# A hybrid attention, convolution and FFN layer on one core: rows of the normed input at one address remainder, halves of 272 + 256 and 258 columns, and another order of loads

## The chip, the cores and the metric

One Trainium2 chip, one core. The metric is the device time of one execution in microseconds. Times of before are the median, lowest and highest of 3 runs. The profiled execution is a run of its own, with a time of its own.

## The reference, cut to what matters

One decoder layer on 512 tokens of width 2048, all in float32. 16 meta tokens stand in front, so the input stage works on L = 528 columns; the output has the last 512.

```python
n = _rmsnorm(h, g_mix)                       # h: 16 meta tokens + 512 tokens, 2048 wide
q, k, v, gb, gc, u = split(n @ w_in)         # six parts of 1024
o_attn = stick_breaking(rmsnorm(q), rmsnorm(k), v)     # 8 heads of 128
o_conv = gb * causal_dwconv(gc * u, conv_w)            # 3 taps, 1024 channels
h = h + concat(rmsnorm(o_attn), rmsnorm(o_conv)) @ w_out
n2 = _rmsnorm(h, g_ffn)
h = h + (silu(n2 @ w_gate) * (n2 @ w_up)) @ w_down     # 5632 wide
return h[:, 16:]
```

## The kernel before, in words

Everything is kept transposed: channels on the 128 partitions, tokens along a row. Each float32 operand is split into a high and a low float32r part, and each product is three matmuls, high·high, high·low, low·high. ScalarE and VectorE make the parts of the weights (`split_quad`, L188 and L189: `s_buf` from `w_buf`) a few quads ahead of their use; SyncE loads `w_buf` (`load_at`, L172) as places come free. The order of everything is the order in which the program is written, with three exceptions: `after(n, work)` puts work behind n further k-tiles (`tick` counts them down), `tc.high_priority` moves work ahead, and a tile is written only when the readers of what lay in its place are through.

**x.** `split_x` (L347) writes for each of 16 k-tiles two tiles of 128 x 528, `nh` and `nl`, with one row of 2112 bytes per partition each.

**Heads.** For each of 8 heads the products k, q and v are made by `product_steps` (L280, L282, L284): k and v over all 528 columns as two matmuls of 264 (H = L // 2, one per PSUM bank), q over 512 (names pk, pq, pv). The first k and q (`pk0`, `pq0`) are made while x is still being loaded and split. `qk_norm` and `attend` are put behind some k-tiles of later products.

**Convolution.** Two of the eight conv heads (CONV_FIRST = 2) are made in the plain way: c and u (pcu) as two matmuls of 260 columns, b (pb) as one of 512. Their results are stored to DRAM (`od`). The other six go by a 2 x 2 block scheme with seven products rather than eight: `form_blocks` makes four mixed blocks of x and stores them in DRAM (`fc`), with blocks of 8 k-tiles x CH = 260 columns (two 260s from column C0 = 8). Three of them are loaded into `blk` (L701), the fourth over columns 268 to 527 of the first 8 k-tiles of `nh` and `nl` (L708), all by GpSimd's queue. `pair_product` then makes, for each pair of heads and each of c, u and b, seven block products of 8 k-tiles x 3 matmuls (L742 to L744): y from n, x from `blk`, z from `blk`, x from `blk`, and z, x, x from n. `conv_taps` and `conv_out` finish on VectorE and ScalarE.

**Output projection.** `wide_product` (L842 to L844, po) reads `oc` (conv) and `oa` (attention), 512 columns at a time. The six conv heads of the block scheme lie in SBUF: four in `oc_mid`, the last two in places 0 and 1 of `oc_end`. The first two conv heads and the eight attention heads are loaded from `od` by GpSimd (L812), the conv ones into places 2 and 3 of `oc_end`. `scale_c` (its sums over partitions are `ss_c`, L636 and L637) makes the conv group's norm and is put behind 3 k-tiles of the first product.

**FFN.** The residual's norm gives blocks f0 to f6, each 8 k-tiles x 256 columns, high and low, in rows of 1024 bytes. f3, f4 and f6 go through DRAM (`fx`): they are stored tile by tile (L991, L997), and at the last tile 7 of their 8 k-tiles are loaded back, f6 in two halves by SyncE (L977), f3 and then f4 in two halves each by GpSimd (L980). f4 lies in a pool of its own (`fpool_4`), f3 and f6 in another (`fpool_last`), both where tiles of the output projection lay. Then come 44 pairs of gate and up, seven products each (y from f5, x f0, z f1, x f2, z f3, x f4, x f6, L742 to L744), and the down projection of the same form from `first` and `ring`.

Of the kernel before, what the change touches and what calls it, by code (L numbers as in the profile page):

```python
# [33 lines left out]
def hybrid_layer(ctx: ExitStack, tc: tile.TileContext, xT, w_in, w_out, w_gu, w_down, vecs, out):  # L34
# [23 lines left out]
    sm = open_pool("sm", 4, space=PSUM)  # L58

# [262 lines left out]
    H = L // 2  # L322
    n_hl = []
# [6 lines left out]
    def x_scale():  # L330
        ve.tensor_tensor(acc, acc, accs[1], ALU.add)
        for a in (0, H):
            ps = small(f"ssx{a}")
            pe.matmul(ps[:, :H], ones, acc[:, a : a + H], start=True, stop=True)
            ve.tensor_scalar(ms[:, a : a + H], ps[:, :H], 1.0 / D, EPS, ALU.mult, ALU.add)
# [11 lines left out]
    def split_x(k):  # L347
        nh = npool.tile([P, L], F32R, tag=f"nh{k}", name=f"nh{k}")
        nl = npool.tile([P, L], F32R, tag=f"nl{k}", name=f"nl{k}")
        g = g_mix[:, k : k + 1]  # L350
        sc.activation(nh, xts[k], AF.Copy, scale=g)
        ve.scalar_tensor_tensor(nl, xts[k], g, nh.bitcast(F32), ALU.mult, ALU.subtract)
        n_hl.append((nh, nl))

    def square_x(k):
# [55 lines left out]
    C0, CH = 8, (L - 8) // 2  # L411
    fc = dram.tile([P, 4, 2, 8, CH], F32R, name="fc")

    def form_blocks(k):

        x4 = stage.tile([P, 4, CH], F32, tag="x4", name=f"x4_{k}")
        st = stage.tile([P, 8 * CH], F32R, tag="st", name=f"st4_{k}").rearrange("p (i a t) -> p i a t", i=4, a=2)
        for i, kk in ((0, k), (2, k + 8)):
            nc.sync.dma_start(x4[:, i : i + 2], two(xT[kk][:, C0:]))
# [26 lines left out]
    def qk_norm(ps, g, cols, dst, parts_of, name):  # L446
# [33 lines left out]
    def head(h):  # L480

        if h:
            pk = pp.tile([P, 2, 512], F32, tag="pp", name=f"pk{h}")
            product([(pk[:, 0, :H], 0, H), (pk[:, 1, :H], H, L)], n_hl)
        else:
            pk = pk0
        kn = kns[0]
        kh = apool.tile([P, 384], F32R, tag="kh", name=f"kh{h}")
        kl = apool.tile([P, 384], F32R, tag="kl", name=f"kl{h}")
        after(8 if h else 11, qk_norm(halves(pk, H), g_k, L, kn[:, :L], (kh, kl, 384), f"k{h}"))  # L490
# [12 lines left out]
        product([(pv[:, 0, :H], 0, H), (pv[:, 1, :H], H, L)], n_hl)  # L503
        vt = t512(L, "e", 2)
        ve.tensor_tensor(two(vt[:, :L]), halves(pv, H), two(r), ALU.mult)
        after(6 if h else 11, lambda: attend(h, kn, kh, kl, qn, qh, ql, vt))
# [146 lines left out]
    def conv_taps(j, c1, c2, y):  # L653

        ve.tensor_tensor(c1, c1, two(r2[:, C0:]), ALU.mult)
        ve.tensor_tensor(c1, c2, c1, ALU.mult)
        cu = c1.rearrange("p a b -> p (a b)")
        o = META - 2 - C0
        sc.activation(y, cu[:, o : o + SEQ], AF.Copy, scale=cw[:, 3 * j : 3 * j + 1])
        for t in (1, 2):  # L660
            ve.scalar_tensor_tensor(
                y, cu[:, o + t : o + t + SEQ], cw[:, 3 * j + t : 3 * j + t + 1], y, ALU.mult, ALU.add
            )
# [12 lines left out]
    for j in range(CONV_FIRST):  # L676
# [14 lines left out]
        if j == 0:  # L691
# [14 lines left out]
    for k in range(8):  # L706
        for part in range(2):
            gp.dma_start(n_hl[k][part][:, C0 + CH :], fc[:, 1, part, k])  # L708

    def parts_of(kk, a):  # L710
        return lambda part, k: n_hl[kk + k][part][:, a : a + CH]

    def of_blk(i):
        return lambda part, k: blk[:, i, part, k]

    conv_acts = [
        parts_of(0, C0), of_blk(2), of_blk(0), of_blk(1), parts_of(0, C0 + CH), parts_of(8, C0), parts_of(8, C0 + CH)
# [69 lines left out]
    def pair(acts):  # L787
        c1, c2 = halves_of("e"), halves_of("e2")
# [4 lines left out]
    for j in range(CONV_FIRST, HEADS, 2):  # L793
        ys = []
        for m in range(2):
            c1, c2 = pair(conv_acts)
            ys.append(t512(SEQ, "v", 2)[:, :SEQ])
            conv_taps(j + m, two(c1), two(c2), ys[m])
        gbs = pair(conv_acts)
        if j < HEADS - 2:  # L800
            slots = [oc_mid[:, j + m - CONV_FIRST] for m in range(2)]
        else:
# [3 lines left out]
            oc_end = o_slots(oc2_pool, "oc_end", 4)  # L806
# [71 lines left out]
    after(3, scale_c)  # L878
# [26 lines left out]
    for i, j in enumerate(OUT_TILES):  # L905
# [35 lines left out]
        if i == KT - 1:  # L941
# [292 lines left out]
```

## Time and profile before

| what | value |
|---|---|
| median of 3 runs | 2044.49 us (2041.42 to 2046.47) |
| profiled execution, its time | 2048.55 us |
| profiled execution, its span | 2046.8 us |
| its mean granted TensorE clock | 0.998 |
| PE busy | 2032.0 us, 99% of the span, 16158 instructions |
| DVE, ACT, POOL busy | 84%, 51%, 19% |
| DMA | 361.70 MB, mean 177 GB/s |

How to read it: the span is the profiled work, and the execution's own time has 1.75 us around it. Matmuls overlap in the array, so a record of one lasts longer than the step from one start to the next; the step is what the time is made of. A PEclk of 1.00 is 2.4 GHz and 0.50 is 1.2 GHz.

### The profile page before, as it was taken

Reading aid. Unit: us, or ns where it says so; the run is one execution under the profiler, and the core shown is the slowest. Engines: PE = TensorE matmul, PEld = TensorE weight load, DVE = VectorE, ACT = ScalarE, POOL = GpSimd, SP = SyncE. Lnnn points to the kernel's source line nnn. Section 1 sums busy time; section 2 is a strip of 40 time slices with the busy share of each in tenths; the row PEclk is TensorE's granted clock in tenths of the full one; section 3 lists DMA queues with packets and bytes.
Section 4 is the critical chain, followed back from the end, with each engine's and each line's share of the span. In section 5 each row is a group of like instructions: output and inputs, shape, how many; then the busy total and the mean of one; then the engine's idle time right before and its main releaser. Section 6 shows DMA issues by size and latency. Waiting matters only on the chain.

```text
span 2046.8 us, 39727 instructions
## 1 busy us (share of the span) xinstructions
PE 2032.0 (99%) x16158; PEld 1969.1 (96%) x16158; DVE 1718.8 (84%) x2202; ACT 1051.1 (51%) x1517; POOL 381.2 (19%) x533
## 2 busy tenths in 40 slices
PE   9999999999999999999999999999999999999999
PEld 8999999999998888999999999999999999999999
DVE  8788878588876777998998998998998998888887
ACT  7666666344443435545555545554554544444443
POOL 0111111210015441011111111111101252223111
PEclk9999999999999999999999999999999999999999
DMA  6333344743365556566565565555555999989864
GB/s 230 100 129 116 127 138 130 254 149 104 104 211 181 184 181 205 155 174 171 150 176 150 151 175 153 154 171 158 151 174 152 274 311 314 246 237 255 231 156 89
DMA packets 161591, 361.70 MB, mean 177 GB/s; under 512 B 13568, under 2 KB 73216, under 8 KB 161408
## 3 DMA queue, kind: packets, MB, share of 16 engines
q1 hardware_dynamic: 79200, 227.94, 34.8%
q0 software_dynamic: 82208, 131.23, 24.4%
q8 instruction: 127, 2.08, 0.4%
q14 instruction: 56, 0.46, 0.1%
HBM read 278.50 MB, written 80.61 MB: 175 GB/s over the span
## 4 chain that ended last, share of the span: by engine, by line
PE 92%; DVE 3%; ACT 2%; DMA 2%; issue 2%; POOL 1%; SPq 0%; DVEq 0%; ACTq 0%; POOLq 0%
PE x L742 13%; PE x L744 13%; PE x L743 13%; PE z L742 6%; PE z L743 6%; PE z L744 6%; PE y L743 3%; PE y L742 3%; PE y L744 3%; PE po L843 2%; PE po L842 2%; PE po L844 2%; PE pv L280 2%; PE pv L284 1%; PE pv L282 1%
## 5 line engine op out<-in xcount | busy, mean ns | idle before, releaser
L188 ACT CAST s_buf<-w_buf 128x1024 fp32r<-128x1024 f32 (+2 forms) x665 | 660.5, 993 | 772.6 <-PE x L743 348.7
L189 DVE TENSOR_TENSOR s_buf<-w_buf,s_buf 128x1024 fp32r<-128x1024 f32 (+2 forms) x665 | 767.8, 1155 | 173.9 <-ACT s_buf L188 173.4
L743 PE MATMUL x<-f,s_buf 128*128 128x256 f32 x1408 | 388.5, 276 | 4.2 <-DMA f<-fx 4.2
L742 PE MATMUL x<-f,s_buf 128*128 128x256 f32 x1408 | 388.5, 276 | 0.5 <-ACT sides L772 0.5
L744 PE MATMUL x<-f,s_buf 128*128 128x256 f32 x1408 | 388.4, 276 | 0.0
L201 DVE TENSOR_TENSOR w_buf<-w_buf 128x1024 f32<-128x1024 f32 (+1 forms) x243 | 277.6, 1142 | 14.2 <-DMA w_buf<-w_in 9.9
L743 PEld LDWEIGHTS x<-f,s_buf 128*128 128x128 f32 x1408 | 265.4, 188 | 4.4 <-DMA f<-fx 4.4
L742 PEld LDWEIGHTS x<-f,s_buf 128*128 128x128 f32 x1408 | 265.3, 188 | 1.2 <-ACT sides L772 0.9
L744 PEld LDWEIGHTS x<-f,s_buf 128*128 128x128 f32 x1408 | 265.4, 188 | 0.0
L1036 POOL DMA_DIRECT2D fd<-s x147 | 104.0, 926 | 713.0 <-DVE s L295 691.8
L742 PE MATMUL z<-f,s_buf 128*128 128x256 f32 x704 | 193.6, 275 | 0.0
L743 PE MATMUL z<-f,s_buf 128*128 128x256 f32 x704 | 193.6, 275 | 0.0
L744 PE MATMUL z<-f,s_buf 128*128 128x256 f32 x704 | 193.6, 275 | 0.0
L744 PE MATMUL x<-ring,s_buf 128*128 128x256 f32 x608 | 167.3, 275 | 0.9 <-DVE s_buf L189 0.9
L742 PE MATMUL x<-ring,s_buf 128*128 128x256 f32 x608 | 167.2, 275 | 0.0
L743 PE MATMUL x<-ring,s_buf 128*128 128x256 f32 x608 | 167.2, 275 | 0.0
L744 PEld LDWEIGHTS z<-f,s_buf 128*128 128x128 f32 x704 | 132.1, 188 | 0.0
L743 PEld LDWEIGHTS z<-f,s_buf 128*128 128x128 f32 x704 | 132.1, 188 | 0.0
L742 PEld LDWEIGHTS z<-f,s_buf 128*128 128x128 f32 x704 | 132.1, 188 | 0.0
L1106 POOL DMA_DIRECT2D out_T<-d x62 | 60.3, 1002 | 300.4 <-DVE d L1114 240.7
L744 PEld LDWEIGHTS x<-ring,s_buf 128*128 128x128 f32 x608 | 114.1, 188 | 1.1 <-DVE s_buf L189 1.1
L743 PEld LDWEIGHTS x<-ring,s_buf 128*128 128x128 f32 x608 | 114.1, 188 | 0.0
(378 smaller groups left out, 5259.4 us busy)
## 6 DMA issues: line engine op xcount, KB each, us to landing
w_buf<-w_gu SPq DMA_DIRECT2D x176, 512.0 KB, 3.4
w_buf<-w_in SPq DMA_DIRECT2D x92, 512.0 KB, 3.4
fd<-s POOLq DMA_DIRECT2D x147, 256.0 KB, 5.2
w_buf<-w_down SPq DMA_DIRECT2D x96, 384.0 KB, 4.9
ring<-fd POOLq DMA_DIRECT2D x42, 768.0 KB, 9.1
w_buf<-w_out SPq DMA_DIRECT2D x32, 512.0 KB, 3.6
out_T<-d POOLq DMA_DIRECT2D x62, 256.0 KB, 5.6
fc<-st SPq DMA_DIRECT2D x8, 1040.0 KB, 6.2
```

Source lines behind the costliest of these rows:

```text
L188: sc.copy(hi, src)
L189: in_turn(ve.tensor_tensor(lo, src, hi.bitcast(F32), ALU.subtract), turn)
L201: in_turn(ve.tensor_tensor(sums[name], a, b, ALU.add), turn)
L280: pe.matmul(ps, wh, ah[:, a:b], start=k == 0, stop=False)
L742: pe.matmul(p, hi[:, kk], act(0, k), start=start and j == k == 0, stop=False, skip_group_check=skip)
L743: pe.matmul(p, hi[:, kk], act(1, k), start=False, stop=False, skip_group_check=skip)
L744: pe.matmul(p, lo[:, kk], act(0, k), start=False, stop=k == n - 1, skip_group_check=skip)
L842: pe.matmul(ps, hi[:, kk], ah, start=k == order[0], stop=False)
L843: pe.matmul(ps, hi[:, kk], al, start=False, stop=False)
L844: pe.matmul(ps, lo[:, kk], ah, start=False, stop=k == order[-1])
L1036: gp.dma_start(fd[c][s][:, :, k], t[:, :, i])
L1106: gp.dma_start(two(out[j]), c, accum_op=ALU.add)
```

## The change

- **One tile for the two rows of x.** `split_x` makes one tile per k-tile, of 2 x 576 columns; high and low rows of 530 columns stand in it from column 12, so they are 2304 bytes apart and all 32 rows have the same address modulo 256 bytes.
- **k and v in 272 + 256 columns.** H = 272 rather than 264. `row_of` puts the two pieces next to each other across the two PSUM banks, so that `qk_norm` and `attend` read one row of 528 (before: two of 264).
- **Conv blocks of 258 columns.** C0 = 14 and C1 = 270, CH = 258: two halves that overlap by 2 columns. c and u are made in 258 columns, b in the last 256 of them (`last_of`). `blk` has rows of 288 columns, high and low next to each other (1152 bytes apart; 2304 from k-tile to k-tile), and is loaded in runs of 1032 bytes, not 4160. `form_blocks` loads x in four pieces of 258, not two of 520. `conv_taps` multiplies by `r2` in two operations of 258 (before: one of 520).
- **The loads of two conv results.** `oc_end` is two tiles: `oc_end` (the last two block heads) and `oc_01` (the first two heads, loaded from `od`). `scale_c` is put behind 13 k-tiles, not 3.
- **The loads of f3 and f6.** SyncE loads k-tiles 0 to 5 of f3 ahead of f6; GpSimd loads k-tile 6 of f3 alone, then f4.
- The scratch memory for descriptors of GpSimd's DMAs is 8192 bytes, not 16384.

The diff, cut to its core:

```diff
-    H = L // 2
+    H, ROW = META + T2, 2304 // 4
...
-        nh = npool.tile([P, L], F32R, tag=f"nh{k}", name=f"nh{k}")
-        nl = npool.tile([P, L], F32R, tag=f"nl{k}", name=f"nl{k}")
+        n = npool.tile([P, 2 * ROW], F32R, tag=f"n{k}", name=f"n{k}")
+        n_row = n.rearrange("p (a t) -> p a t", a=2)[:, :, 12 : 14 + L]
+        nh, nl = (n_row[:, i, :L] for i in range(2))
...
+    def row_of(ps):
+
+        flat = ps.rearrange("p a b -> p (a b)")
+        return flat[:, 512 - H : 512 - H + L], [(flat[:, 512 - H : 512], 0, H), (flat[:, 512 : 512 + L - H], H, L)]
...
-    C0, CH = 8, (L - 8) // 2
+    C0 = META - 2
+    C1, CH = C0 + T2, L - C0 - T2
...
-            product([(pk[:, 0, :H], 0, H), (pk[:, 1, :H], H, L)], n_hl)
+            product(row_of(pk)[1], n_hl)
...
-        ve.tensor_tensor(c1, c1, two(r2[:, C0:]), ALU.mult)
+        for m, c in enumerate((C0, C1)):
+            ve.tensor_tensor(c1[:, m], c1[:, m], r2[:, c : c + CH], ALU.mult)
...
-            product([(p[:, 0, :CH], C0, C0 + CH), (p[:, 1, :CH], C0 + CH, L)], n_hl)
+            product([(p[:, 0, :CH], C0, C0 + CH), (p[:, 1, :CH], C1, L)], n_hl)
...
-            blk = blk_pool.tile([P, 3, 2, 8, CH], F32R, name="blk")
-            for i, n in ((2, 3), (0, 0), (1, 2)):
+            blk = blk_pool.tile([P, 8 + 48 * 288], F32R, name="blk")
+            blk = blk[:, 2 : 2 + 48 * 288].rearrange("p (i k a t) -> p i k a t", i=3, k=8, a=2)
+            pad(blk_pool, 128)
+            for i, n in enumerate((3, 0, 2)):
                 for part in range(2):
-                    gp.dma_start(blk[:, i, part], fc[:, n, part], max_dma_last_dim=4160)
+                    gp.dma_start(blk[:, i, :, part, :CH], fc[:, n, part])
...
-            gp.dma_start(n_hl[k][part][:, C0 + CH :], fc[:, 1, part, k])
+            gp.dma_start(n_rows[k][:, part, C0 + CH :], fc[:, 1, part, k])
...
-        gbs = pair(conv_acts)
+        gbs = pair([last_of(act) for act in conv_acts], T2)
...
-            oc_end = o_slots(oc2_pool, "oc_end", 4)
+            oc_end = o_slots(oc2_pool, "oc_end", 2)
+            oc_01 = o_slots(oc2_pool, "oc_01", CONV_FIRST)
...
-    after(3, scale_c)
+    after(13, scale_c)
...
-            for part in range(2):
-                nc.sync.dma_start(acts[6][:, part, :7].bitcast(F32), fx[6][:, part, :7].bitcast(F32), max_dma_last_dim=4096)
-            for s in (3, 4):
-                for part in range(2):
-                    gp.dma_start(acts[s][:, part, :7], fx[s][:, part, :7], max_dma_last_dim=4096)
+            for s, n in ((3, 6), (6, 7)):
+                for part in range(2):
+                    nc.sync.dma_start(acts[s][:, part, :n].bitcast(F32), fx[s][:, part, :n].bitcast(F32), max_dma_last_dim=4096)
+            gp.dma_start(acts[3][:, :, 6], fx[3][:, :, 6])
+            for part in range(2):
+                gp.dma_start(acts[4][:, part, :7], fx[4][:, part, :7], max_dma_last_dim=4096)
...
-    nc = bacc.Bacc("TRN2", target_bir_lowering=False, num_devices=1)
+    nc = bacc.Bacc("TRN2", target_bir_lowering=False, num_devices=1, dynamic_dma_scratch_size=8192)
```

GpSimd's queue at the end of the output projection, before; `w227` and `w229` are the residual's last two tiles, `st6` the last mixed blocks, `fd` a later stage:

```order
L1000 DMA out_T<-w223_7761 128x512
L314 TENSOR_TENSOR acc_h_6624<-acc_h_6624,w226_7785 128x512
L900 DMA w229_7822<-xT 128x512
L997 DMA fx3_6636<-st6_7780 256x1x256
L997 DMA fx4_6637<-st6_7780 256x1x256
L980 DMA f3_7935<-fx3_6636 128x2x896 x2
L980 DMA f4_7925<-fx4_6637 128x2x896 x2
L1036 DMA fd0_0_7962<-s0_2_8211 256x1x256
```

The same place after the change:

```order
L1017 DMA out_T<-w223_7767 128x512
L317 TENSOR_TENSOR acc_h_6630<-acc_h_6630,w226_7791 128x512
L916 DMA w229_7828<-xT 128x512
L1014 DMA fx3_6642<-st6_7786 256x1x256
L1014 DMA fx4_6643<-st6_7786 256x1x256
L995 DMA f3_7941<-fx3_6642 128x2x256
L997 DMA f4_7931<-fx4_6643 128x2x896 x2
L1053 DMA fd0_0_7969<-s0_2_8218 256x1x256
```

Two large loads of f3 have left this queue; one small one stands in their place, and the two loads of f4 follow it.

SyncE's queue at that place, before (the rows are its loads of weights, of f6 and two stores of the output):

```order
L172 DMA w_buf_111<-w_gu 128x1024 x4
L977 DMA f6_7936<-fx6_6638 128x2x896 x2
L1000 DMA out_T<-w227_7817 128x512
L172 DMA w_buf_111<-w_gu 128x1024
L1000 DMA out_T<-w229_7822 128x512
```

And after the change:

```order
L175 DMA w_buf_111<-w_gu 128x1024 x4
L994 DMA f3_7941<-fx3_6642 128x2x768 x2
L994 DMA f6_7942<-fx6_6644 128x2x896
L1017 DMA out_T<-w227_7823 128x512
L175 DMA w_buf_111<-w_gu 128x1024
L994 DMA f6_7942<-fx6_6644 128x2x896
L1017 DMA out_T<-w229_7828 128x512
```

The two loads of f3 stand ahead of f6 here, and the second half of f6 has moved behind an output store and a load of weights.

TensorE at the end of the first product of the output projection, before; `ss_c` is the conv group's sum of squares:

```order
L842 MATMUL po0_6639<-oc_end_6582,s_buf_112 128x512
L843 MATMUL po0_6639<-oc_end_6582,s_buf_112 128x512
L844 MATMUL po0_6639<-oc_end_6582,s_buf_112 128x512
L842 MATMUL po0_6639<-oc_end_6582,s_buf_112 128x512
L636 MATMUL ss_c_6660<-w167_6654,ones_r_107 128x512
L843 MATMUL po0_6639<-oc_end_6582,s_buf_112 128x512
```

After the change:

```order
L863 MATMUL po0_6645<-oc_01_6588,s_buf_112 128x512
L861 MATMUL po1_6646<-oc_end_6587,s_buf_112 128x512
L862 MATMUL po1_6646<-oc_end_6587,s_buf_112 128x512
L863 MATMUL po1_6646<-oc_end_6587,s_buf_112 128x512
L649 MATMUL ss_c_6696<-w167_6690,ones_r_107 128x512
L650 MATMUL ss_c_6696<-w168_6691,ones_r_107 128x512
L861 MATMUL po1_6646<-oc_end_6587,s_buf_112 128x512
```

`ss_c` has moved back by five matmuls: it stood within the last k-tile of po0, and now stands behind the first k-tile of po1.

## Rows read from the trace of the kernel before

**Rows 1.** The page's busy time by engine, whole span.
```profile
PE 2032.0 (99%) x16158; PEld 1969.1 (96%) x16158; DVE 1718.8 (84%) x2202; ACT 1051.1 (51%) x1517; POOL 381.2 (19%) x533
```

**Rows 2.** Waits of PE: who waited for what, us in total, times, longest us.
```profile
PE x L743 <- DMA f<-fx: 4.2, 1, 4.2
...
PE ss_c L636 <- ACT w L294: 1.1, 1, 1.1
PE x L744 <- DVE s_buf L189: 1.1, 2, 0.9
```

**Rows 3.** PE by windows (length, busy, records): pk, pq, pcu, pairs, po, FFN.
```profile
221.12:228.12 7.00, 7.00 (x60) 1.00 0.87 273
231.55:234.32 2.77, 2.77 (x14) 1.00 0.56 189
381.29:388.50 7.21, 7.21 (x62) 1.00 0.90 305
449.09:466.37 17.28, 17.28 (x147) 1.00 0.33 116
699.67:763.00 63.33, 63.33 (x281) 1.00 0.58 177
1000.02:1600.02 600.00, 600.00 (x5297) 1.00 0.55 159
```

**Rows 4.** PE's timeline where the pq window starts: start, duration, instruction.
```profile
231.29 0.29 PE L584 MATMUL c<-bh,ones_r 128*128 128x288 f32 x1
231.42 0.29 PE L585 MATMUL c<-bl,ones_r 128*128 128x288 f32 x1
231.55 0.40 PE L280 MATMUL pq<-nh,s_buf 128*128 128x512 f32 x1
```

**Rows 5.** The chain of waits around the loads of f3 and f4.
```profile
774.98 0.45 POOL f L980
...
777.13 16.11 DMA f<-fx
793.28 0.58 PE x L743
```

**Rows 6.** Windows behind that wait: length, PE, PEld, DVE, ACT, POOL, PEclk, DMA, GB/s.
```profile
793.28:798.35 5.07, 5.07 (x23) 5.07 (x24) 0.00 (x0) 0.00 (x0) 0.00 (x0) 0.50 0.29 103
798.35:799.13 0.78, 0.78 (x3) 0.64 (x3) 0.42 (x1) 0.71 (x1) 0.00 (x0) 0.57 0.00 0
```

**Rows 7.** DMA, 763 to 794 us: rate; then queue, count, KB, us to landing.
```profile
DMA packets 3229, 9.38 MB, mean 303 GB/s; under 512 B 240, under 2 KB 752, under 8 KB 3227
...
f<-fx POOLq DMA_DIRECT2D x4, 896.0 KB, 11.1
...
f<-fx SPq DMA_DIRECT2D x2, 896.0 KB, 8.3
```

**Rows 8.** The chain of waits, 600 to 610 us, around ss_c.
```profile
605.48 1.31 POOL acc_c L314
...
606.81 0.63 ACT w L294
...
607.48 0.50 PE ss_c L636
607.98 0.23 PE po L843
```

**Rows 9.** Windows, columns as in rows 6: loads of blk, of n, conv pairs.
```profile
382.00:405.00 23.00, 23.00 (x191) 22.91 (x190) 12.31 (x15) 7.70 (x12) 4.70 (x7) 1.00 1.02 368
405.00:416.00 11.00, 11.00 (x50) 8.98 (x50) 5.61 (x6) 3.09 (x5) 8.49 (x16) 1.00 1.01 236
416.00:600.00 184.00, 183.23 (x1520) 182.37 (x1519) 152.23 (x167) 88.02 (x118) 15.41 (x15) 1.00 0.37 122
```

**Rows 10.** DMA, 407 to 416 us, as in rows 7: loads of n.
```profile
DMA packets 2242, 2.26 MB, mean 251 GB/s; under 512 B 251, under 2 KB 2186, under 8 KB 2241
...
nh<-fc POOLq DMA_DIRECT2D x7, 130.0 KB, 3.2
```

More of the change, by code (lines that the diff above doesn't have):

```diff
@@ L332, in x_scale @@
         for a in (0, H):
-            ps = small(f"ssx{a}")
-            pe.matmul(ps[:, :H], ones, acc[:, a : a + H], start=True, stop=True)
-            ve.tensor_scalar(ms[:, a : a + H], ps[:, :H], 1.0 / D, EPS, ALU.mult, ALU.add)
+            b = L if a else H
+            ps = small(f"ssx{a}")[:, : b - a]
+            pe.matmul(ps, ones, acc[:, a:b], start=True, stop=True)
+            ve.tensor_scalar(ms[:, a:b], ps, 1.0 / D, EPS, ALU.mult, ALU.add)
         rsqrt(r, ms, L)
@@ L418, in form_blocks @@
         for i, kk in ((0, k), (2, k + 8)):
-            nc.sync.dma_start(x4[:, i : i + 2], two(xT[kk][:, C0:]))
+            for m, c in enumerate((C0, C1)):
+                nc.sync.dma_start(x4[:, i + m], xT[kk][:, c : c + CH])
         for i, kk in ((0, k), (2, k + 8)):
@@ L455, in qk_norm @@
         cuts = [(0, cols)] if cols == SEQ else [(0, H), (H, L)]
-        raw_v, s_v = (raw, s) if cols == SEQ else (two(raw), two(s))
-        sc.activation(s_v, ps, AF.Square)
-        sc.activation(raw_v, ps, AF.Copy, scale=g)
+        sc.activation(s, ps, AF.Square)
+        sc.activation(raw, ps, AF.Copy, scale=g)
         split(sh, sl, s)
@@ L489, in head @@
         kl = apool.tile([P, 384], F32R, tag="kl", name=f"kl{h}")
-        after(8 if h else 11, qk_norm(halves(pk, H), g_k, L, kn[:, :L], (kh, kl, 384), f"k{h}"))
+        after(8 if h else 11, qk_norm(row_of(pk)[0], g_k, L, kn[:, :L], (kh, kl, 384), f"k{h}"))
         if h:
@@ L502, in head @@
         pv = pp.tile([P, 2, 512], F32, tag="pp", name=f"pv{h}")
-        product([(pv[:, 0, :H], 0, H), (pv[:, 1, :H], H, L)], n_hl)
+        pv_row, parts = row_of(pv)
+        product(parts, n_hl)
         vt = t512(L, "e", 2)
-        ve.tensor_tensor(two(vt[:, :L]), halves(pv, H), two(r), ALU.mult)
+        ve.tensor_tensor(vt[:, :L], pv_row, r, ALU.mult)
         after(6 if h else 11, lambda: attend(h, kn, kh, kl, qn, qh, ql, vt))
@@ L653, in conv_taps @@
     def conv_taps(j, c1, c2, y):
-        ve.tensor_tensor(c1, c1, two(r2[:, C0:]), ALU.mult)
+        for m, c in enumerate((C0, C1)):
+            ve.tensor_tensor(c1[:, m], c1[:, m], r2[:, c : c + CH], ALU.mult)
         ve.tensor_tensor(c1, c2, c1, ALU.mult)
-        cu = c1.rearrange("p a b -> p (a b)")
-        o = META - 2 - C0
-        sc.activation(y, cu[:, o : o + SEQ], AF.Copy, scale=cw[:, 3 * j : 3 * j + 1])
+        y = two(y)
+        sc.activation(y, c1[:, :, :T2], AF.Copy, scale=cw[:, 3 * j : 3 * j + 1])
         for t in (1, 2):
             ve.scalar_tensor_tensor(
-                y, cu[:, o + t : o + t + SEQ], cw[:, 3 * j + t : 3 * j + t + 1], y, ALU.mult, ALU.add
+                y, c1[:, :, t : t + T2], cw[:, 3 * j + t : 3 * j + t + 1], y, ALU.mult, ALU.add
             )
@@ L707, in hybrid_layer, with last_of @@
         for part in range(2):
-            gp.dma_start(n_hl[k][part][:, C0 + CH :], fc[:, 1, part, k])
+            gp.dma_start(n_rows[k][:, part, C0 + CH :], fc[:, 1, part, k])
     def parts_of(kk, a):
-        return lambda part, k: n_hl[kk + k][part][:, a : a + CH]
+        return lambda part, k: n_rows[kk + k][:, part, a : a + CH]
     def of_blk(i):
-        return lambda part, k: blk[:, i, part, k]
+        return lambda part, k: blk[:, i, k, part, :CH]
+    def last_of(act):
+        return lambda part, k: act(part, k)[:, CH - T2 :]
     conv_acts = [
-        parts_of(0, C0), of_blk(2), of_blk(0), of_blk(1), parts_of(0, C0 + CH), parts_of(8, C0), parts_of(8, C0 + CH)
+        parts_of(0, C0), of_blk(0), of_blk(1), of_blk(2), parts_of(0, C0 + CH), parts_of(8, C0), parts_of(8, C1)
     ]
@@ L785, in pair_product, with pair @@
         return x
-    def pair(acts):
-        c1, c2 = halves_of("e"), halves_of("e2")
+    def pair(acts, n):
+        c1, c2 = (halves_of(t)[:, : 2 * n] for t in ("e", "e2"))
         x = pair_product(acts, two(c1), two(c2), sides)
@@ L810, in hybrid_layer @@
             with tc.high_priority():
-                for name, t in [(f"c{m}", oc_end[:, 2 + m]) for m in range(2)] + [(f"a{h}", oa_all[:, h]) for h in range(HEADS)]:
+                for name, t in [(f"c{m}", oc_01[:, m]) for m in range(2)] + [(f"a{h}", oa_all[:, h]) for h in range(HEADS)]:
                     gp.dma_start(t, od[name])
         for m in range(2):
-            s = t512(SEQ, "e", 2)[:, :SEQ] if j == HEADS - 2 else cpool.tile([P, SEQ], F32, tag="s", name=f"sq{j}_{m}")
+            s = t512(SEQ, "e", 2)[:, :SEQ] if j == HEADS - 2 else gbs[m]
             with tc.high_priority(1 << 20) if j == HEADS - 2 else ExitStack():
-                conv_out(j + m, gbs[m][:, META - C0 :], ys[m], slots[m][:, 0], slots[m][:, 1], s, ve)
-    oc = [oc_end[:, 2], oc_end[:, 3], *(oc_mid[:, i] for i in range(HEADS - 2 - CONV_FIRST)), oc_end[:, 0], oc_end[:, 1]]
+                conv_out(j + m, gbs[m], ys[m], slots[m][:, 0], slots[m][:, 1], s, ve)
+    oc = [oc_01[:, 0], oc_01[:, 1], *(oc_mid[:, i] for i in range(HEADS - 2 - CONV_FIRST)), oc_end[:, 0], oc_end[:, 1]]
     oc_order = (*range(CONV_FIRST, HEADS), *range(CONV_FIRST))
```

11 lines of the change are left out of this document (6 added, 5 removed).

## The prediction

> **What bounds the kernel now.** I read four views in this order. First the busy times: PE is busy for 2032.0 of 2046.8 us [rows 1], so the time is what TensorE's steps take, and only 14.8 us are left to win from its pauses. Then PE's waits: one stands out, 4.2 us for the load of an FFN block; the next two, 1.1 us for `ss_c` and 1.1 us for a weight split, are small [rows 2]. Then the length of a step, which the mean duration of a record can't show, since records overlap; I read it from windows cut at the start of a matmul and ending at the start of another [rows 3]. A window also counts the records still running at its start: at 231.55 the two of 231.29 and 231.42, 0.29 long each, are still open [rows 4], so its 14 records are 12 steps. With two off each: pk 7.00 us / 58 = 120.7 ns for 264 columns, pq 2.77 / 12 = 230.8 for 512, pcu 7.21 / 60 = 120.2 for 260, the conv pairs 17.28 / 145 = 119.2 for 260, po 63.33 / 279 = 227.0 for 512, the FFN 600.00 / 5295 = 113.3 for 256.
>
> The reader is to see that these are two rates at one granted clock of 1.00. The FFN takes 113.3 / 256 = 0.443 ns a column, po 0.443, and at that rate 264 columns take 116.9, 260 take 115.1, 512 take 226.7. All products that read `nh`, `nl` or `blk` are 3.8 to 5.1 ns a step above it. What sets these apart in the code is the row of the moving operand: f rows of 1024 bytes and oa, oc rows of 2048 are whole multiples of 256 bytes, rows of 2112 (n) and 1040 (blk) are not, so there the address modulo 256 changes from matmul to matmul. That the remainder is the cause is my inference; no row of before varies it alone.
>
> Last the chain of waits and the windows around the 4.2 us, which hold more than the wait itself.
>
> **The rows of x and the widths.** Steps that the change touches, counted from the loops:
>
> - k and v: 8 heads x 2 products x 16 k-tiles x 3 x 2 pieces = 1536, less the first k (96), made while x still comes in: 1440. At 272 + 256 the mean is 264 as before. Full gain 120.7 - 116.9 = 3.8 ns, 5.5 us. But the two pieces start at columns 0 and 272, 1088 bytes apart, so two remainders 64 bytes apart still alternate. Between no gain and 5.5 I take half, 2.7 us.
> - q: 384 less 48 in the start, and b of two heads, 96: 432 steps of 512. All start at one remainder now. 230.8 - 227.0 = 3.8 ns, 1.6 us, taken whole, since po shows the rate at this width.
> - plain c, u: 384 steps, 120.2 to 258 x 0.443 = 114.2: 6.0 ns, 2.3 us, taken whole; columns 14 and 270 lie 1024 bytes apart.
> - conv pairs: 9 pair products x 7 blocks x 24 = 1512 steps. Six of nine have 258 columns (1008 steps, 119.2 - 114.2 = 5.0 ns), three have 256 (504, 5.9 ns): 8.0 us in full. Four of seven blocks read n rows: 4.6 us, taken whole. Three of seven read `blk`, where high and low rows lie 1152 bytes apart, 128 modulo 256: at most 3.4 us, of which 0.8 is columns alone; I take that and half of the rest, 2.1.
>
> Sum: 2.7 + 1.6 + 2.3 + 4.6 + 2.1 = 13.3 us; bounds 2.1 us (columns alone: (384 x 2 + 1008 x 2 + 504 x 4) x 0.443 ns) and 17.4.
>
> The Trainium skill speaks against this term: "SBUF — State Buffer", section "Who interferes with whom", gives TensorE two read ports of its own, for the moving operand and for the weights, and says that it waits on nobody; then address would not matter. By that rule the sum would be 2.1. The trace disagrees: 512 columns took 230.8 ns from n and 227.0 from oa.
>
> **The loads of f3 and f4.** GpSimd issues f3 and f4 from 774.98 on; the transfer ends at 793.28, and PE has waited 4.2 us, so f4 was wanted at 789.1 [rows 2, 5]. Behind the wait TensorE is granted 0.50 for 5.07 us and 0.57 for 0.78 [rows 6]: of the 26 steps there, 24 of 256 columns and 2 of 512 take 24 x 0.1133 + 2 x 0.227 = 3.17 us at full clock, so 5.85 - 3.17 = 2.7 us more. A pause of 4.2 us went ahead of that fall of the clock. Together 6.9 us.
>
> Before, 4 x 896 KB = 3.67 MB went through GpSimd's queue, in 18.3 us from the first issue to 793.28; at the stretch's 303 GB/s [rows 7] 5.5 MB moved in that time, so about 1.9 MB were others'. After, GpSimd has 256 + 2 x 896 KB = 2.1 MB. With the same 1.9 MB beside it that is 13.2 us, landing at about 788.4, 0.7 us ahead of need. f3's first six k-tiles ride ahead of f6 on SyncE's queue, and its seventh is the first thing GpSimd sends. SyncE's queue then holds 2 x 768 + 896 - 2 x 896 = 640 KB more ahead of its next load of weights, 2.2 us at that rate; splits are made some quads ahead, which hides it; without that cover it costs those 2.2 us. f6's second half moves behind one load of weights; f6 is the last block to be read. I take 6.6 us of 6.9; the ends are 3 us (f4 lands 3 us late and the clock still falls in part) and 7.1.
>
> **The loads of two conv results and ss_c.** PE waits 1.1 us for the chain acc_c 1.31, square root and scale 0.63 [rows 2, 8]. After the change `ss_c` stands 5 matmuls of 0.227 later, 1.1 us. I take 0.9, ends 0.3 and 1.3. The separate `oc_01` lets its loads be issued without waiting for readers of `oc_end`'s place; nothing on PE waits for them in the rows, so nothing is counted.
>
> **Small edits.** `r2` in two operations: 8 more on VectorE, each under the mean there of 152.23 / 167 = 0.91 us, so under 7.3 us in all; VectorE idles 184 - 152.23 = 31.8 us in the six block heads [rows 9]. Nothing counted; without that cover up to 0.5 us per pair. `form_blocks` issues 16 more loads on SyncE, whose bytes do not grow, and is early. PSUM rows in one piece: nothing.
>
> **blk in runs of 1032 bytes.** Before, the six loads ran at 368 GB/s, and n's 16 loads, of runs near 1 KB, at 236 to 251 [rows 9, 10]. Now all are of that kind: 6.2 MB of blk, 2.1 of n and about 3 of others are 11.3 MB at 251 GB/s = 45 us from 382, ending at 427. The first block, y, starts where the last of these windows does, at 416, and takes 24 steps; x from `blk` follows at about 419, when 6.2 MB and a third of the others' bytes, 29 us' worth, should be in (411). n's new columns are first read after four blocks (4 x 24 x 0.119 = 11.4 us), at 427.4 or a little later. Cost 0, up to 4 if the rate is lower.
>
> **Sum.** 13.3 + 6.6 + 0.9 = 20.8 us off the profiled execution's 2048.55: 2027.8. That execution stands 4.06 us above the median of the three runs, so on the median 2023.7, say **2024**.
>
> **Rivals.**
> (1) *All moved rows reach the fast rate*, k, v and blk too, 17.4 + 6.9 + 1.3 = 25.6: 2019. For: one alternation of two remainders may do no harm; against: in rows 3 nothing with two remainders is fast. Chance 0.18.
> (2) *Only width counts.* The rate belongs to something other than the address, say to the splits going on beside it; then columns alone, 2.1 + 6.6 + 0.9 = 9.6: 2035. For: pq and po differ in more than the address. Against: po, pq and pcu run beside splits alike. Chance 0.17.
> (3) *blk or n comes late*, by up to 4 us, and the clock falls by part: 20.8 - 4 to 7 us, 2028 to 2031. Chance 0.08.
> (4) *Slower: GpSimd's descriptors.* Half the scratch memory might let one load's descriptors fit in place of two, so that its queue goes one load at a time: descriptors, transfer, landing in a row. Then each blk load costs its 1040 KB at 251 GB/s, 4.2 us, plus up to 6 of the rest, six of them 63 us, and 16 of n about 3.7 us each, 60: the n rows come at 382 + 63 + 60 = 505 rather than 430, 75 us late, and the time is about 2100. It decides from the point where the 22 loads take over 48 us. For: runs four times shorter want four times the descriptors; against: GpSimd is busy only 4.70 of the 23 us of blk's loads [rows 9]. Chance 0.04.
> (5) *The load doesn't move.* f4 still waits for the readers of its place and f3's late piece, and 4 us of the 6.9 stay: 2028. Inside the range; it is part of the forecast's chance.
>
> **How the numbers follow.** Forecast 0.53, rivals (1) to (4) 0.18, 0.17, 0.08, 0.04. The range takes in (1) with its lower bound, three us below for the scatter of the median, 2016, and (2) with 1 us above, 2036; outside lie (4) and the tails, under 0.2. A measurement of this kernel can tell 0.3%, 6.1 us, from no change. (2) at -9.6 with a partly kept f4 wait comes to -6: a third of it counts as same, 0.06. Slower is (4) and one more unseen wait, 0.05. Faster 0.89.
>
> **What would show it.** Right: windows over pk near 119 ns a step, pq at 227, pcu at 114.2, conv pairs from n at 114.2 and from blk near 117; no wait for f<-fx above 1 us and a granted clock of 1.00 through 788 to 800 us (some 14 us earlier by then); no wait at ss_c. Wrong: pq still at 230.8 (then the address is not the cause), steps from blk slower than from n before, a new PE wait for blk or n<-fc near 420 to 433 us, or gaps between GpSimd's loads there.

## The result and the profile after

The changed kernel takes 2051.84 us in the median of 7 runs (2049.41 to 2053.15), the kernel before 2044.49 in 7 runs beside them (2040.53 to 2047.78): ratio 1.0035, 95% interval 1.0025 to 1.0044. It is slower by 7.35 us where 20 us of gain were forecast. The profiled execution of the change took 2049.81, 2.0 under its median; that of before took 2048.55, 4.06 above its own. The two profiles are therefore only 1.3 us apart, and a comparison of them alone misleads.

The page's busy times of the change answer to [rows 1]:

```profile
span 2048.1 us, 39799 instructions
...
PE 2032.1 (99%) x16158; PEld 1963.7 (96%) x16158; DVE 1720.4 (84%) x2210; ACT 1049.1 (51%) x1517; POOL 382.1 (19%) x532
```

PE is as busy as before. Its waits in the change (us in total, times, longest) answer to [rows 2]:

```profile
PE ss_k L477 <- ACT sh_k L297: 2.5, 3, 1.0
PE c L601 <- DVE spl L298: 2.3, 8, 0.6
PE x L762 <- DVE s_buf L192: 1.2, 2, 1.0
...
PE ss_k L478 <- DVE sl_k L298: 1.1, 3, 0.4
PE c L600 <- ACT sph L297: 0.9, 1, 0.9
...
PE ss_c L650 <- DVE w L298: 0.2, 1, 0.2
```

The wait for f4 is gone and that at `ss_c` is down to 0.2, as forecast. New or longer are waits within the attention heads, for what ScalarE and VectorE make of k and of the sums: 2.5, 2.3, 1.1 and 0.9 us.

To see where the time went, the starts of four stretches are read from the views of the tiles `pv`, `y` and `ring` (line, count, shortest, median and longest ns, first and last start). Before, in that order: the first v product, the first conv pair, the first FFN pair, the first down product:

```profile
L280 PE MATMUL pv<-nh,s_buf x32: 281/285/479, 31.8 to 45.1; 128*128 128x264 f32 x32
L742 PE MATMUL y<-nh,s_buf x8: 281/282/285, 415.9 to 418.4; 128*128 128x260 f32 x8
L742 PE MATMUL y<-f,s_buf x8: 275/275/281, 775.1 to 777.5; 128*128 128x256 f32 x8
L742 PE MATMUL x<-ring,s_buf x608: 275/275/275, 1622.1 to 2042.4; 128*128 128x256 f32 x152
```

After:

```profile
L283 PE MATMUL pv<-n,s_buf x32: 277/284/476, 29.8 to 43.1; 128*128 128x272 f32 x16, 128*128 128x256 f32 x16
L760 PE MATMUL y<-n,s_buf x8: 278/283/287, 424.9 to 427.4; 128*128 128x258 f32 x8
L760 PE MATMUL y<-f,s_buf x8: 275/275/281, 782.3 to 784.7; 128*128 128x256 f32 x8
L760 PE MATMUL x<-ring,s_buf x608: 275/275/275, 1622.5 to 2043.7; 128*128 128x256 f32 x152
```

| stretch | before | after | difference |
|---|---|---|---|
| heads and two plain conv heads (pv to first conv pair) | 384.1 | 395.1 | +11.0 |
| block conv heads and output projection (to first FFN pair) | 359.2 | 357.4 | -1.8 |
| gate and up (to first down product) | 847.0 | 840.2 | -6.8 |

The heads lost 11 us. The gate and up stretch got back what the wait for f4 and the low clock cost in that one profile of before. The table adds up to 2.4 us; the start in front of it is 2.0 us shorter (31.8 to 29.8; a second profile of before has 30.6, so it scatters by itself) and the down projection 0.9 longer, which leaves the 1.3 us between the two spans.

The step lengths answer to [rows 3], windows cut at starts as there, with the records still running at the start, and one that only starts at the end, taken off again (k 60 steps, pb 48, conv pairs 144, po 12):

```profile
224.87:232.25 7.38, 7.38 (x63) 1.00 0.95 272
413.79:424.88 11.09, 11.09 (x51) 1.00 1.22 298
424.88:442.29 17.41, 17.41 (x145) 1.00 0.57 169
700.13:702.85 2.72, 2.72 (x14) 1.00 0.26 98
```

k takes 123.0 ns a step in this stretch (before 120.7 in its own), pb 231.0 for 512 columns, the first conv pairs 120.9 for 258, po 226.7. None of these reads of x's rows became faster, although all rows now share one remainder modulo 256. Whole pair products of the conv, 168 steps each, show more; one of c and u before, in 260 columns:

```profile
436.49:456.59 20.10, 20.10 (x170) 1.00 0.31 100
```

and after, one of c and u in 258 columns and one of b in 256:

```profile
445.63:465.89 20.26, 20.26 (x170) 1.00 0.33 101
465.89:485.55 19.66, 19.66 (x171) 1.00 0.32 100
```

That is 119.6 ns a step before, 120.6 and 117.0 after: b gained, c and u lost, and all nine pair products together take 181.5 us rather than 182.6.

The heads' new waits begin on another engine. ScalarE's waits for x's loads, 31 to 377 us, before:

```profile
ACT x L421 <- DMA x<-xT: 2.6, 6, 0.6
```

and after:

```profile
ACT x L434 <- DMA x<-xT: 13.1, 5, 3.5
```

One of the five, in the timelines of the change (start, duration, instruction, idle time before it and its releaser). SyncE:

```profile
133.49 0.52 SPq L441 DMA_DIRECT2D fc<-st  x1
134.07 3.71 SPq L432 DMA_DIRECT2D x<-xT  x4
```

ScalarE:

```profile
143.35 0.73 ACT L434 ACTIVATE x<-x,vec 128x516 f32<-128x516 f32 x1 [3.52 <-DMA x<-xT]
143.98 0.53 ACT L297 CAST sph<-sp 128x432 fp32r<-128x432 f32 x1
```

PE:

```profile
150.72 0.39 PE L477 MATMUL ss_k<-sh_k,ones_r 128*128 128x272 f32 x1 [0.95 <-ACT sh_k L297]
151.47 0.39 PE L478 MATMUL ss_k<-sl_k,ones_r 128*128 128x272 f32 x1 [0.35 <-DVE sl_k L298]
151.70 0.28 PE L477 MATMUL ss_k<-sh_k,ones_r 128*128 128x256 f32 x1
151.82 0.28 PE L478 MATMUL ss_k<-sl_k,ones_r 128*128 128x256 f32 x1
```

ScalarE works in order: while it stands 3.52 us before x's rows for the mixed blocks, `sph` of the attention and later `sh_k` of k's norm wait behind it, and PE arrives at `ss_k` first. The list of PE's waits shows only part of the loss, 7.5 us from 29 to 425 us against 0.9 before, since a record outlasts its step and idle time counts from the record's end: from 150.72 to 151.47 pass 0.75 us, of which 0.35 count as idle, where the step at 151.70 takes 0.12.

SyncE issues x's loads right behind the store of the previous mixed block. That store is what the list of DMA issues shows changed (queue, count, KB, median us to landing); before:

```profile
fc<-st SPq DMA_DIRECT2D x8, 1040.0 KB, 6.2
```

and after:

```profile
fc<-st SPq DMA_DIRECT2D x8, 1032.0 KB, 7.8
```

It moves fewer bytes and lands 1.6 us later. The loads of x behind it land later too, though each has half the bytes of before (260.0 KB in 6.0 us):

```profile
x<-xT SPq DMA_DIRECT2D x28, 129.0 KB, 6.6
```

### The profile page after: what moved, and what is told of

Same layout as the page of the kernel before. It is cut to its first block, busy times and chain, and to the rows that moved or that the text cites. A ratio compares the mean times of both kernels' runs of the same rounds, so it can differ in the third digit from the quotient of the medians.

```text
span 2048.1 us, 39799 instructions
## 1 busy us (share of the span) xinstructions
PE 2032.1 (99%) x16158; PEld 1963.7 (96%) x16158; DVE 1720.4 (84%) x2210; ACT 1049.1 (51%) x1517; POOL 382.1 (19%) x532
## 4 chain that ended last, share of the span: by engine, by line
PE 88%; DVE 4%; ACT 3%; issue 2%; DMA 1%; POOL 1%; SPq 0%; DVEq 0%; ACTq 0%; POOLq 0%
PE x L762 13%; PE x L760 13%; PE x L761 13%; PE z L762 7%; PE z L760 6%; PE z L761 6%; PE y L762 3%; PE y L761 3%; PE y L760 3%; PE po L861 3%; PE po L863 3%; PE po L862 3%; PE pv L283 1%; PE pv L285 1%; PE pv L287 1%
## 6 DMA issues: line engine op xcount, KB each, us to landing
w_buf<-w_down SPq DMA_DIRECT2D x96, 384.0 KB, 4.9
```

## The experiments

**The kernel before, a second profile.** No edit.

> The kernel before, unchanged, for a second profile. Theory S (the wait for f4 and the low clock behind it are in some executions of before only): this profile, if its time is near the median of 2044.5 or below, shows a wait for f4 of under 2 us and a granted clock of 1.00 behind it. Rival (the wait is in every execution, and the scatter of 2040.5 to 2047.8 lies elsewhere): again a wait near 4.2 us and a clock near 0.50 for some 5 us behind it, whatever the time.

2041.77 us. PE waits 1.0 us for f4, and the clock stays up. The windows of all engines from 780 to 800 us (length, PE, PEld, DVE, ACT, POOL, PEclk, DMA share, GB/s), first profile of before:

```profile
780.00:800.00 20.00, 15.80 (x113) 15.44 (x112) 12.98 (x19) 7.25 (x11) 0.00 (x0) 0.83 0.70 256
```

and this one:

```profile
780.00:800.00 20.00, 19.02 (x165) 18.74 (x164) 18.62 (x23) 10.61 (x16) 0.00 (x0) 1.00 0.66 245
```

Theory S holds: the wait of 4.2 us and the granted clock near 0.50 belong to some executions of the kernel before. Its 16 runs beside this profile sort the same way: the eleven up to 2043.59 us have a mean granted clock of 1.000, the five from 2044.27 to 2048.85 one of 0.998 or 0.999.

**x's rows in two loads of one run.** The first theory of the loss in the heads.

```diff
-            for m, c in enumerate((C0, C1)):
-                nc.sync.dma_start(x4[:, i + m], xT[kk][:, c : c + CH])
+            nc.sync.dma_start(x_row[:, i * CH + 2 : (i + 2) * CH], xT[kk][:, C0:])
```

> The change, but x's rows for the mixed blocks are loaded again in two loads of one run of 2056 bytes per partition, not in four of 1032; ScalarE cuts the overlapping halves out of them (four operations of 258 columns, not two of 516). Theory L (the four loads land too late, ScalarE stands in its order behind them for 13.1 us in all, and TensorE then waits for what ScalarE has behind them): ScalarE's wait for x falls from 13.1 us to under 4, the products from the third head to the last plain conv head come out 9 to 11 us shorter, the time is 2041 to 2043. Rival K (the loss of the heads is in k and v themselves: 272 + 256 columns in one PSUM row across two banks, and the norms that read it): nothing changes there, 2051 to 2053.

2049.21 us (2047.97 to 2051.06), ratio to before 1.003 (1.0018 to 1.0041). ScalarE's wait for x is 13.2 us in 5 waits, unchanged. Theory L falls: the number of loads is not it. Rival K is no better: its 2051 to 2053 was missed too, and the wait stays on x's loads. What had not been undone was the store ahead of the loads: it lands in 7.5 us here.

**Only the loads of the change.** The kernel before with f3 on SyncE, `oc_01` of its own and `scale_c` behind 13 k-tiles.

```diff
-            oc_end = o_slots(oc2_pool, "oc_end", 4)
+            oc_end = o_slots(oc2_pool, "oc_end", 2)
+            oc_01 = o_slots(oc2_pool, "oc_01", CONV_FIRST)
...
-    after(3, scale_c)
+    after(13, scale_c)
...
+            for s, n in ((3, 6), (6, 7)):
+                for part in range(2):
+                    nc.sync.dma_start(acts[s][:, part, :n].bitcast(F32), fx[s][:, part, :n].bitcast(F32), max_dma_last_dim=4096)
+            gp.dma_start(acts[3][:, :, 6], fx[3][:, :, 6])
```

> The kernel before with only the loads of the change: f3's first six k-tiles on SyncE ahead of f6, f4 next on GpSimd, oc_01 as a tile of its own, scale_c behind 13 k-tiles. The forecast's term (6.6 us for f4, 0.9 for ss_c, in the median of before too): 7.5 us faster, 2037, and no wait for f4 above 1 us. Theory S (the wait is in some executions only): 3 to 5 us faster, 2040 to 2041, with a narrower scatter than before's 7 us. Rival (the load of f3 on SyncE costs as much elsewhere): no change, 2044.

2039.74 us in 11 runs, 2039.25 to 2040.79; the kernel before beside it 2042.98 in 16 runs, 2040.51 to 2048.85; ratio 0.998 (0.9971 to 0.9989). Theory S again: 3.2 us in the median, and the scatter falls from 8.3 us to 1.5, which fits an upper tail of before that was this wait; PE has no wait for f4 in this profile.

**Other rows under the output projection.** Attention rows 2304 and 2112 bytes apart, in place of 2048.

```diff
-            oa_all = o_slots(oapool, "oa", HEADS)
+            for n, c in ((0, 576), (4, 528)):
+                t = oapool.tile([P, 8 * c], F32R, name=f"oa{n}_").rearrange("p (h a t) -> p h a t", h=4, a=2)
+                oa_rows += [t[:, h, :, :SEQ] for h in range(4)]
```

> The change, but the attention rows of the output projection are spaced otherwise: heads 0 to 3 with 2304 bytes from row to row (one remainder modulo 256 bytes, four modulo 1024), heads 4 to 7 with 2112 bytes, as x's rows had before (four remainders modulo 256); the conv rows stay at 2048 and are the control. Now all take 227 ns a step of 512 columns. Theory A256 (the forecast: one remainder modulo 256 is the fast case): heads 0 to 3 stay at 227, heads 4 to 7 go to 231. Theory A1024 (only one remainder modulo 1024 or more is fast): both go to 231. Theory N (the address does not matter): both stay at 227. The control stays at 227 in all three.

One execution, 2053.64 us. One product (po8), PE's windows of heads 0 to 3 and of heads 4 to 7, 12 steps each:

```profile
698.45:701.17 2.72, 2.72 (x13) 1.00 0.61 205
701.17:703.96 2.79, 2.79 (x13) 1.00 0.57 204
```

226.7 ns at a spacing of 2304, 232.5 at 2112: the forecast's inference holds here, one remainder modulo 256 is fast and four are not. Theories A1024 and N fall. The control moved, though: the first conv rows behind the slow ones took up to 236 ns for about ten steps, so a disturbed stream needs some steps to settle. The puzzle is then why x's rows, 2304 apart as well, stay at 231. By the places that the program gives them, q's and b's rows begin at 240 modulo 256, the attention rows at 128.

**Rows that begin at a multiple of 64 bytes.**

```diff
-        n_row = n.rearrange("p (a t) -> p a t", a=2)[:, :, 12 : 14 + L]
+        n_row = n.rearrange("p (a t) -> p a t", a=2)[:, :, 16 : 18 + L]
...
-            blk = blk[:, 2 : 2 + 48 * 288].rearrange("p (i k a t) -> p i k a t", i=3, k=8, a=2)
+            blk = blk[:, 6 : 6 + 48 * 288].rearrange("p (i k a t) -> p i k a t", i=3, k=8, a=2)
```

> The change, but x's rows begin 16 columns into their tile rather than 12, and blk's 16 bytes later, so that q's and b's rows begin at a multiple of 64 bytes (0 modulo 256 in n) rather than at 240 modulo 256; the spacing of rows stays. In the changed kernel q takes 231 ns a step although all its rows share one remainder, and in the run with other attention rows po kept 227 with rows 2304 bytes apart that begin at 128 modulo 256. Theory B (one remainder modulo 256 is fast only where rows also begin at a multiple of 64 bytes, unless they are a multiple of 1024 apart): q and pb fall to 227, b's blocks from n from 116.4 to 113.4; that is 432 x 4 + 288 x 3 ns = 2.6 us at most, 2049 rather than 2051.8. Rival P (it lies in the place of x's tiles or in their k-tile spacing of 4608 bytes, not in where a row begins): q stays at 231 and the time at 2051 to 2053.

2050.72 us, ratio 1.0037 (1.0024 to 1.0051). pb took 48 steps in the window

```profile
415.40:426.55 11.15, 11.15 (x51) 1.00 1.17 291
```

or 232.3 ns, no better than 231.0. Theory B falls: a multiple of 64 is not enough. Rival P is left open here.

**Blocks stored and loaded in 272 columns.** The second theory of the loss: rows of 1032 bytes begin in DRAM at any multiple of 8 bytes.

```diff
-    fc = dram.tile([P, 4, 2, 8, CH], F32R, name="fc")
+    FH = META + T2
+    fc_all = dram.tile([P, 4, 2, 8, FH], F32R, name="fc")
+    fc = fc_all[:, :, :, :, C0 : C0 + CH]
...
-            for m, c in enumerate((C0, C1)):
-                nc.sync.dma_start(x4[:, i + m], xT[kk][:, c : c + CH])
+            for m, c in enumerate((0, T2)):
+                nc.sync.dma_start(x4[:, i + m], xT[kk][:, c : c + FH])
```

> The change, but the mixed blocks are formed, stored in DRAM and read from x in 272 columns (rows of 1088 bytes, each beginning at a multiple of 64 bytes in DRAM), still in four loads; the conv reads the same 258 columns of them. Undoing the four loads alone left ScalarE's wait for x at 13.2 us. Theory U (runs of 1032 bytes that begin at multiples of 8 bytes make some packets slow, the longest 0.7 to 0.9 us rather than 0.17, so that the store of the blocks lands 1.5 us later and x's loads behind it on SyncE's queue later still): the store's landing falls from 7.8 to about 6.3 us, ScalarE's wait for x from 13.1 to under 5, the heads are 8 to 10 us shorter, the time is 2041 to 2044. Rival Q (SyncE's queue merely holds more loads, or ScalarE comes earlier to its wait): the wait stays above 10 us and the time above 2048.

2038.66 us (2038.07 to 2039.27), ratio to before 0.9975 (0.9965 to 0.9985). The store, now with more bytes, lands in 6.0 us, and ScalarE's wait for x is

```profile
ACT x L436 <- DMA x<-xT: 3.1, 4, 0.9
```

Theory U holds, though its 2041 to 2044 was not low enough, and this version is faster than both kernels.

**Only the store's beginnings, only x's loads.** The two halves of the edit above, each on the change alone. The store's: rows of 1032 bytes, 1088 apart.

```diff
-    fc = dram.tile([P, 4, 2, 8, CH], F32R, name="fc")
+    fc = dram.tile([P, 4, 2, 8, META + T2], F32R, name="fc")[:, :, :, :, :CH]
```

> The change, but the rows of the stored blocks stand 1088 bytes apart in DRAM, so that each run begins at a multiple of 64 bytes; the runs are still 1032 bytes and x is still loaded in runs of 1032. Storing and loading in 272 columns took the time from 2051.8 to 2038.7; this does the store's half, and only its beginnings. Theory W (the store's runs that begin or end within a 64-byte piece are what is slow): if beginnings count, the store lands in 6 to 6.5 us, ScalarE waits under 6 us for x, and the time is 2039 to 2042; if ends count as well, it stays near 7.5 us and the time near 2050. Rival V (it is x's loads that are slow): no change, 2050 to 2053.

2039.62 us (2038.28 to 2040.58), ratio 0.9978 (0.9968 to 0.9987). Its store in the list of DMA issues:

```profile
fc<-st SPq DMA_DIRECT2D x8, 1032.0 KB, 6.1
```

ScalarE's wait for x:

```profile
ACT x L434 <- DMA x<-xT: 3.2, 6, 0.7
```

Its first conv pair, in the view of the tile `y`:

```profile
L760 PE MATMUL y<-n,s_buf x8: 279/284/288, 414.1 to 416.7; 128*128 128x258 f32 x8
```

Its loads of x behind the store:

```profile
x<-xT SPq DMA_DIRECT2D x28, 129.0 KB, 4.9
```

The same bytes in the same runs land 1.7 us earlier, the loads behind them as well, and the first conv pair starts at 414.1, not at 424.9. The other half loads x in 272 columns and stores as in the change:

```diff
-        x4 = stage.tile([P, 4, CH], F32, tag="x4", name=f"x4_{k}")
+        x_all = stage.tile([P, 4, META + T2], F32, tag="x4", name=f"x4_{k}")
+        x4 = x_all[:, :, C0 : C0 + CH]
...
-                nc.sync.dma_start(x4[:, i + m], xT[kk][:, c : c + CH])
+                nc.sync.dma_start(x_all[:, i + m], xT[kk][:, c : c + META + T2])
```

> The change, but x is loaded for the blocks in runs of 1088 bytes that begin at multiples of 64; the blocks are still formed in and stored as 258 columns, rows of 1032 bytes. Theory W (the store is what is slow): the store still lands in 7.5 to 8 us, ScalarE still waits 10 to 13 us, the time is 2047 to 2052. Rival V (the loads are): the wait falls under 5 us, the time to 2039 to 2042.

2048.86 us (2045.81 to 2049.95), ratio 1.0021 (1.0011 to 1.0031), with this store and this wait of ScalarE:

```profile
fc<-st SPq DMA_DIRECT2D x8, 1032.0 KB, 7.5
```

```profile
ACT x L435 <- DMA x<-xT: 13.4, 5, 4.0
```

Theory W holds: it is the store, and of it the pitch of its rows. What about the pitch is open. At 1088 bytes each run begins at a multiple of 64, at 1032 only at a multiple of 8; but before, 1040 apart, they began at multiples of 16 and landed in 6.2 all the same, and the distance between runs changes with the pitch as well.

**Rows that begin at 128 modulo 256.** x's tiles 128 bytes lower and the rows 16 columns in, on the version in 272 columns.

```diff
+    pad(npool, 128)
     stage = open_pool("stage")
...
-        n_row = n.rearrange("p (a t) -> p a t", a=2)[:, :, 12 : 14 + L]
+        n_row = n.rearrange("p (a t) -> p a t", a=2)[:, :, 16 : 18 + L]
```

> The run with blocks stored in 272 columns, with x's tiles 128 bytes lower and x's rows 16 columns into them, so that q's, pb's and b's rows all begin at 128 modulo 256, as the rows of the output projection do; spacing 2304 bytes as in the change. Seen so far, at a spacing of 2304: 240 modulo 256 gives 231 ns for 512 columns of x, 0 gives 233, 128 gives 227 for attention rows. Theory R (the remainder itself decides, 128 being a good one): q and pb fall to 227, b's 256 columns from n from 116.4 to 113.4, k and v change little; 432 x 4 + 288 x 3 ns = 2.6 us, 2036 against 2038.7. Rival P (the place of x's tiles, higher in the memory, decides): q stays at 231 to 233, the time at 2038 to 2040.

2037.74 us (2037.05 to 2038.6), ratio 0.9974 (0.9964 to 0.9985), the lowest median here. pb's 48 steps, in the version with 272 columns at 240 modulo 256:

```profile
403.51:414.59 11.08, 11.08 (x50) 1.00 1.22 301
```

and at 128:

```profile
402.66:413.54 10.88, 10.88 (x51) 1.00 1.20 298
```

230.8 and 226.7 ns. Theory R holds for rows of 512 columns (the edit moves `blk` by 128 bytes as well, but pb does not read it). It misses on the narrow ones: b's 256 columns from n went from 116.4 to 119.9 ns in the mean of their steps. Not 2.6 us but 0.9 lie between the two medians, and their ratios to before, 0.9975 and 0.9974, can't be told apart.

**Attention rows at 240 and at 0.**

```diff
-            oa_all = o_slots(oapool, "oa", HEADS)
+            for n, c in ((0, 28), (4, 0)):
+                t = oapool.tile([P, 8 * 576 + c], F32R, name=f"oa{n}_")
+                t = t[:, c:].rearrange("p (h a t) -> p h a t", h=4, a=2)
```

> The change, with the attention rows of the output projection 2304 bytes apart; heads 0 to 3 begin at 240 modulo 256, heads 4 to 7 at 0. In the earlier run the same rows at 128 took 227 ns. Theory R (the remainder decides): heads 0 to 3 take 231, as q does from x's rows at 240, heads 4 to 7 take 233, as q did at 0. Rival P (the place decides): both stay at 227.

One execution, 2052.40 us. The same two windows of po8, heads 0 to 3 (240) and 4 to 7 (0):

```profile
697.23:699.99 2.76, 2.76 (x14) 1.00 0.58 209
699.99:702.78 2.79, 2.79 (x13) 1.00 0.61 189
```

230.0 and 232.5 ns, where 128 gave 226.7. Rival P falls: it is not where x's tiles lie; at this spacing and width it is the remainder. It is not the remainder alone: the FFN's rows, 1024 bytes apart, begin at 240 too and take 113.3 ns for 256 columns, where b's rows from n, 2304 apart and at 240, take 116.4.

**k and v in 256 + 272 columns.**

```diff
-    H, ROW = META + T2, 2304 // 4
+    H, ROW = T2, 2304 // 4
```

> The run with blocks stored in 272 columns, with k and v cut into 256 + 272 columns rather than 272 + 256, so that both pieces of a row begin 1024 bytes apart and all rows of k and v share one remainder modulo 256. Now the two take 123.8 to 125.4 and 117.0 ns, 121 in the mean, as in the kernel before. The forecast's step (two alternating remainders keep k and v from the fast rate; with one they reach 117): 1440 x 4 ns = 5.8 us, 2033. Theory R (one remainder is not enough, its value decides, and here it is 176): mean of 119 to 121, at most 2 us, 2037 to 2039.

2039.25 us, ratio 0.9982 (0.9973 to 0.9991), no different from 2038.66. k's window, 60 steps,

```profile
220.74:228.16 7.42, 7.42 (x64) 1.00 0.85 264
```

is 123.7 ns a step; with 272 + 256 columns the same stretch (219.03 to 226.42 us) had 123.2. The forecast's step is missed, and the 119 to 121 that theory R left room for as well: one remainder, of the value 176, gives k and v nothing.

## Why the prediction was wrong

**The step that failed: "`form_blocks` issues 16 more loads on SyncE, whose bytes do not grow, and is early."** It was costed at nothing. It cost 11.0 us in the heads, by way of the store, SyncE's queue, x's loads, ScalarE's order and PE. The forecast looked at the loads and never at the store of the same function, whose rows had gone from 1040 to 1032 bytes. With nothing changed but the rows to 1088 apart the loss is gone, 2051.84 to 2039.62 (ratios to before 1.0035 and 0.9978); with only x's loads changed it stays (1.0021). The sign of a cover that was nearly used up stood in the trace of before: ScalarE already waited for x six times, 2.6 us in all. No row on ScalarE's waits was read.

**The rows of x and the widths: 13.3 us forecast, next to nothing measured.** With the store mended, the whole change stands at 0.9978 of before and its loads alone at 0.998: 0.4 us apart, less than either interval. Their profiles agree stretch by stretch (starts 30.1, 414.1, 771.8, 1611.9 and 29.9, 413.9, 772.5, 1612.7): 384.0 us for the heads in both, 357.7 and 358.6 for the block conv heads and the output projection, 840.1 and 840.2 for gate and up. The inference behind the term, that one remainder modulo 256 is enough, is what failed: with 2304 bytes between rows, 512 columns take 227 ns at 128, 230 to 231 at 240, 232 to 233 at 0. The change put q at 240. The prediction's own sign, pq still at 230.8, came true, but not what it was to mean, that the address is not the cause: moved to 128, the same columns take 226.7. What sets the rate of the narrower products (256 to 272 columns) was not settled: b's pair products fell to 117.0 ns a step, those of c and u rose to 120.6, and k's 123.0 is no better than before. Rival (2), only the columns and 2.1 us, came closest in this part. One reading was off: at the start of the window over the conv pairs three records were open, not two, so its 17.28 us are 144 steps of 120.0 ns and not 119.2, against 119.6 for a whole pair product. The Trainium skill's page "SBUF — State Buffer" ("Who interferes with whom"), with TensorE waiting on nobody, doesn't explain 226.7 against 232.5 ns for the same product at another spacing.

**The loads of f3 and f4: 6.6 us forecast, at most 3.2 measured, together with `ss_c`.** The mechanism was right: the wait is gone, the clock is 1.00, the stretch is 6.8 us shorter than in the first profile of before. But the second profile has 841 us there (its first FFN pair starts at 774.4, its first down product at 1615.5), and the change has 840.2. The step that failed is the last of the sum, where the gain over one profile was carried to the median by taking off 4.06: that profile stood above the median because of this very wait (of the 6.8 us between the two profiles of before 5.9 lie in this stretch), so those microseconds were counted twice. A slip beside it: 2.1 and 1.9 MB at 303 GB/s from 774.98 end at 788.2, not 788.4.

**`ss_c`: right.** 1.1 us of wait fell to 0.2.

**blk in runs of 1032 bytes, and rival (3): right that nothing shows.** PE waits neither for `blk` nor for n's last columns, and GpSimd's queue did not fall behind, so rival (4) did not come either. The rate was taken too low, 251 GB/s (and `blk` has 6.3 MB, not 6.2); while most of `blk` came in, the DMA engines moved 361:

```profile
397.95:413.79 15.84, 15.84 (x133) 1.00 1.62 361
```
The slower side came from a place that no rival named.

## What to carry to other kernels

An edit of a transfer's shape is costed at every transfer of that tensor, the store too, and at what stands behind it on its queue and behind its reader on that engine; how much cover is left is read from the reader's own waits before the edit. When the rows of a DRAM scratch change their length, try their pitch by itself: here 1088 bytes (a multiple of 64) were right for runs of 1032. A stall of one profile is a term only if that profile's time is a typical one: where it stands above the median, profile again before it is counted.

## What the runs showed of the hardware that was not expected

- **The pitch of rows in DRAM.** A store of 1 MB in runs of 1032 bytes landed in 7.8 us (median of 8) when the rows lay 1032 apart, in 6.1 when they lay 1088 apart (one store writes every eighth row); runs of 1040 at a pitch of 1040 landed in 6.2. The Trainium skill's page "DMA: Bandwidth & Descriptors" ("Specifications") asks for transfers of at least 512 bytes for full rate; by that line alone 1032 would do at either pitch, and the trace shows that it does not. Whether it is where a run begins or how far it lies from the next was not tried.
- **The remainder of a moving row.** At one granted clock of 1.00 and the same spacing of 2304 bytes, 512 columns take 226.7, 230.0 or 232.5 ns as the rows begin at 128, 240 or 0 modulo 256, in x's tiles and in the attention rows alike, to within 1 ns. The rule does not reach further: 256 columns at 128 took longer than at 240 (119.9 against 116.4), and at 240 with 1024 bytes between rows 113.3. In one trace, the run with attention rows 2112 apart, about ten steps passed after the slow group before the fast rate was back.
